# Subtracting the low half of the mixing stages' weights on VectorE alone

## The chip, the cores and the metric

The kernel runs on one core of one Trainium2 chip. The metric is the device time of one execution in microseconds (us). TensorE is called PE here, VectorE DVE, ScalarE ACT, GpSimd POOL, and SyncE, which issues most of the transfers, SP.

## The reference

A transformer-like backbone of two layers works on 128 context tokens and 512 latent tokens of width 1024. In each layer one large projection of the normalised input feeds four token mixers (a gated DeltaNet, differential attention, a gated linear recurrence, neighbourhood attention); their outputs are projected, gated, summed and projected again, and a SwiGLU block follows. Everything is float32:

```
h = _rmsnorm(x, lp['norm1_g']) * (1.0 + sc1) + sh1
mix, new_ctx = _token_mixers(h, lp, ctx)          # h @ w_in, four mixers, w_branch, gates, w_out
x = x + g1 * mix
h = _rmsnorm(x, lp['norm2_g']) * (1.0 + sc2) + sh2
x = x + g2 * _swiglu(h, lp['w_ffn_gate'], lp['w_ffn_up'], lp['w_ffn_down'])
```

## The kernel before

Activations lie with features on the 128 partitions and the 640 tokens along the free side, in halves of 320 (`HT`). The operands of the large products are split into a high part `hi` (cast to the type `F32R`) and a low part `lo = x - hi`, and each product is three matmuls: `hi*hi`, `hi*lo`, `lo*hi`.

For a weight this is done in `load_w`: SP issues the load of a tile of 128x1024 into `wraw` (2 buffers), ACT rounds it into `whi` (3 buffers), and the subtraction makes `wlo` (3 buffers). In the mixing stages (`self.weaving` is true) a full tile's subtraction is shared out: 608 columns on DVE, the last 416 (`PC`) on POOL. Everywhere else a full tile is done by DVE alone, but for the first three tiles of the program, which halve it (`pc=512`).

The mixing stage of each layer is woven. PE's instructions stand in an order that a planner writes out (`weave`): it has chains (`mix_a`, `prep_a`, `mix_c`, `mix_d`, `mix_b`, `prep_b`), each a generator that yields where PE has to wait for other engines, and a long list of projections (`fill`: `store_fm`, `store_tok`, `merge`, ...) with which it fills PE until the planner's clock says that a chain is ready. That clock (`now`, `charge`) counts the chains' work on each engine; the weights' subtraction is not counted in it. On DVE, ACT, POOL and SP the order within each engine is set by the framework's scheduler from priorities (`high_priority`; `load_w`'s split has `WPRI` 550000, a chain has 100000 times its rank counted from the back, up to 800000) and its own idea of durations. Each engine then runs its instructions strictly in that order.

Tile names that the text uses: `pu`, `ptk` are products of the projections; `cY`, `cZ`, `cQS`, `cRP`, `cAT`, `pca`, `pcb` belong to chain C (`c_head`); `cacc` is the short convolution of `prep_a`; `GX`, `GT`, `C`, `bm`, `bl`, `pkS`, `xp` belong to chain A; `rx`, `rr` to `prep_b`; `bpr`, `bcx`, `bqt`, `bKd` are loads of chain B that POOL issues; `lmn` is a single number of chain B; names that end in `rs_y` or `rs_t` are steps of a reciprocal root on a few columns. `prep_a`'s and `prep_b`'s transfers and chain B's go through memory, the latter two on POOL's queue.

Of the kernel before, what the change touches and what calls it, by code (L numbers as in the profile page):

```python
# [37 lines left out]
WPRI, WCUT = 550000, 1024  # L38
QB = 1
RE = 0  # L40
PC = 416
DPRI = 0
QM, QD = 1, 0
VC = 1
# [69 lines left out]
class Net:  # L114
# [163 lines left out]
    def load_w(self, src, n=1024, pc=0, raw=None):  # L278

        if raw is None:  # L280
            raw = self.wraw.tile([128, 1024], F32, tag="raw", name="wraw")
        with self.tc.high_priority(offset=DPRI):
            self.nc.sync.dma_start(raw[:, :n], src)
        hi = self.whl.tile([128, 1024], F32R, tag="hi", name="whi")
        lo = self.whl.tile([128, 1024], F32R, tag="lo", name="wlo", bufs=NLO)
        with self.tc.high_priority(offset=WPRI):
            m = n - (PC if self.weaving and n == 1024 else pc)
            self.a.copy(hi[:, :n], raw[:, :n])
            self.v.tensor_tensor(lo[:, :m], raw[:, :m], hi[:, :m].bitcast(F32), ALU.subtract)
            if m < n:  # L290
                self.g.tensor_tensor(lo[:, m:n], raw[:, m:n], hi[:, m:n].bitcast(F32), ALU.subtract)
        return hi, lo
# [1664 lines left out]
```

## Time and profile before

| | |
|---|---|
| median of 3 runs | 3494.56 us (3494.28 to 3498.4) |
| the profiled execution | 3495.59 us, of which 3493.6 us is the span from its first to its last instruction |
| PE busy | 3368.8 us (96%) |
| DVE busy | 2352.5 us (67%) |
| ACT busy | 1422.4 us (41%) |
| POOL busy | 544.5 us (16%) |
| mean granted clock of PE | 0.984 |

The mixing stage of the first layer lies from about 60 to 1240 us, that of the second from about 1780 to 3000 us; between and behind them stand the output projection and the SwiGLU blocks, in which POOL does nothing. PE is the engine to watch: its busy time is nearly the span, so a change shows where PE's idle time, or its time at the lower of its two clock levels (1.2 instead of 2.4 GHz, a granted clock of 0.5), grows or shrinks.

### The profile page before, as it was taken

The numbers are of one execution on the slowest core, as the hardware profiler recorded it, in microseconds if no ns is written. First come the engines' busy times: TensorE is split into PE (matmuls) and PEld (weight loads), VectorE is DVE, ScalarE is ACT, GpSimd is POOL, SyncE is SP. The second block draws the span as 40 slices with busy tenths as digits, with TensorE's granted clock in tenths as the row PEclk, the third lists the DMA queues.
The fourth block names the chain that finished last, engine by engine and source line by source line (L and its number), as shares of the span: only waits on it lengthen the run. The fifth ranks groups of instructions, "written<-read, shape, count | busy, mean of one in ns | idle before, by whom it ended". The sixth has DMA issues, their size and how long they took to land. (4 is left out here: it accounts for less than half of the span.)

```text
span 3493.6 us, 63588 instructions
## 1 busy us (share of the span) xinstructions
PE 3368.8 (96%) x23932; PEld 3298.6 (94%) x23932; DVE 2352.5 (67%) x5497; ACT 1422.4 (41%) x3170; POOL 544.5 (16%) x592
## 2 busy tenths in 40 slices
PE   8999999989999999999999999999999999999998
PEld 5989999988999999999999899999999999999998
DVE  7689888865676478887456797777555646633435
ACT  5344444544543353222253455445544433522222
POOL 2221112422122100000002212124122121000000
PEclk9999999999999999999999999999999999999999
DMA  6444333855454254444244333348453235322222
GB/s 218 151 145 139 115 110 124 242 178 159 131 154 126 95 177 147 151 153 131 76 131 148 130 115 112 103 127 244 141 150 120 87 100 161 106 67 79 74 84 67
DMA packets 297931, 460.16 MB, mean 132 GB/s; under 512 B 48148, under 2 KB 193172, under 8 KB 297624
## 3 DMA queue, kind: packets, MB, share of 16 engines
q1 hardware_dynamic: 286296, 423.58, 39.3%
q0 software_dynamic: 11328, 32.52, 3.1%
q8 instruction: 189, 3.10, 0.4%
q14 instruction: 118, 0.97, 0.1%
HBM read 368.42 MB, written 87.56 MB: 131 GB/s over the span
## 5 line engine op out<-in xcount | busy, mean ns | idle before, releaser
L152 PE MATMUL pu<-hh,whi 128*128 128x320 f32 (+1 forms) x3760 | 1094.7, 319 | 18.1 <-ACT stg L107 14.9
L152 PE MATMUL pu<-hl,whi 128*128 128x320 f32 (+1 forms) x3760 | 1064.8, 311 | 2.2 <-DVE hl L107 2.2
L152 PE MATMUL pu<-hh,wlo 128*128 128x320 f32 (+1 forms) x3760 | 1065.2, 311 | 0.0
L107 ACT CAST whi<-wraw 128x1024 fp32r<-128x1024 f32 (+2 forms) x410 | 391.1, 954 | 898.0 <-PE pu L152 492.6
L152 PEld LDWEIGHTS pu<-hh,whi 128*128 128x128 f32 (+1 forms) x3760 | 683.9, 189 | 23.3 <-ACT stg L107 15.7
L152 PEld LDWEIGHTS pu<-hl,whi 128*128 128x128 f32 (+1 forms) x3760 | 684.3, 189 | 4.5 <-DVE hl L107 2.5
L152 PEld LDWEIGHTS pu<-hh,wlo 128*128 128x128 f32 (+1 forms) x3760 | 682.5, 188 | 1.7
L107 DVE TENSOR_TENSOR wlo<-wraw,whi 128x608 fp32r<-128x608 f32 (+3 forms) x410 | 389.7, 951 | 314.2 <-ACT whi L107 309.4
L107 POOL TENSOR_TENSOR wlo<-wraw,whi 128x416 fp32r<-128x416 f32 (+1 forms) x209 | 325.5, 1558 | 1761.1 <-ACT whi L107 1539.8
L152 PE MATMUL pu<-mo,whi 128*128 128x320 f32 x1024 | 236.5, 318 | 5.4 <-DVE mo L107 3.4
L152 PE MATMUL pu<-fa,whi 128*128 128x320 f32 x1152 | 215.6, 309 | 0.0
L107 DVE SCALAR_TENSOR_TENSOR x<-pu,gn,x 128x128 f32<-128x128 f32 (+1 forms) x336 | 133.8, 435 | 93.3 <-PE pu L152 92.4
L152 PE MATMUL ptk<-whi,hh 128*128 128x256 f32 x640 | 193.9, 303 | 0.0
L512 DVE CUSTOM_DVE_ANT_0 junk<-wa,cs,mod 128x256 bf16<-128x256 f32 (+1 forms) x288 | 172.7, 600 | 25.6 <-DMA wa<-in_wada 20.7
L152 PE MATMUL ptk<-wlo,hh 128*128 128x256 f32 x640 | 183.5, 287 | 3.2 <-DVE wlo L107 3.2
L152 PE MATMUL ptk<-whi,hl 128*128 128x256 f32 x640 | 183.4, 287 | 0.0
L152 PEld LDWEIGHTS pu<-mo,whi 128*128 128x128 f32 x1024 | 174.5, 193 | 7.6 <-DVE mo L107 4.9
L152 PEld LDWEIGHTS pu<-fa,whi 128*128 128x128 f32 x1152 | 180.8, 188 | 0.0
L152 PE MATMUL pu<-mo,wlo 128*128 128x320 f32 x512 | 160.7, 314 | 0.0
L152 PE MATMUL pu<-fa,wlo 128*128 128x320 f32 x576 | 131.1, 309 | 0.0
L152 PEld LDWEIGHTS ptk<-wlo,hh 128*128 128x128 f32 x640 | 125.2, 196 | 3.4 <-DVE wlo L107 3.4
L152 PEld LDWEIGHTS ptk<-whi,hh 128*128 128x128 f32 x640 | 125.5, 196 | 0.0
(422 smaller groups left out, 6092.1 us busy)
## 6 DMA issues: line engine op xcount, KB each, us to landing
wraw<-in_win SPq DMA_DIRECT2D x151, 512.0 KB, 3.9
wa<-in_wada SPq DMA_DIRECT2D x116, 256.0 KB, 3.0
wraw<-in_wg SPq DMA_DIRECT2D x44, 512.0 KB, 3.5
wraw<-in_wu SPq DMA_DIRECT2D x44, 512.0 KB, 3.7
wraw<-in_wd SPq DMA_DIRECT2D x80, 256.0 KB, 2.6
p<-stg SPq DMA_DIRECT2D x112, 160.0 KB, 2.9
wa<-in_wada SPq DMA_DIRECT2D x128, 128.0 KB, 2.5
wraw<-in_wtok SPq DMA_DIRECT2D x32, 512.0 KB, 3.8
```

The source lines that it names most:

```text
L107: r = f(*args, **kw)
L152: r = self.nc.tensor.matmul(out, lhsT, rhs, start=start, stop=stop)
L512: self.nc.vector.tensor_tensor_reduce(junk, raw, cs[g], 0.5, o if k0 else self.bada[:, l, m:m + 1], ALU.mult, ALU.add, o)
```

## The change

The 416 columns go from POOL to DVE: in the mixing stages, DVE now subtracts all 1024 columns of a full tile in one instruction.

```
-PC = 416
...
-            m = n - (PC if self.weaving and n == 1024 else pc)
+            m = n - pc
             self.a.copy(hi[:, :n], raw[:, :n])
             self.v.tensor_tensor(lo[:, :m], raw[:, :m], hi[:, :m].bitcast(F32), ALU.subtract)
             if m < n:
                 self.g.tensor_tensor(lo[:, m:n], raw[:, m:n], hi[:, m:n].bitcast(F32), ALU.subtract)
```

207 instructions leave POOL, and 207 on DVE grow from 608 to 1024 columns. PE's order is the same, instruction for instruction. The scheduler, which counts a longer DVE instruction, orders the others anew: of 5499 instructions on DVE 1295 stand at another place (most by one to five places), of 2748 on ACT 300, of 1715 on SP 340.

POOL in the second layer, where it loads for the fourth head of chain B (`wlo` are the weights' low parts, the DMAs are issues of that head's loads). Before:

```order
313 L163 DMA bqt<-bqk_104 64x4x128 x2
314 L107 TENSOR_TENSOR wlo<-wraw,whi 128x416 x3
315 L163 DMA bqt<-bqk_104 64x4x128 x2
316 L107 TENSOR_TENSOR wlo<-wraw,whi 128x416 x5
317 L107 MEMSET bpr 128x256
318 L163 DMA bcx<-qk_97 128x128
319 L163 DMA bpr<-qk_97 64x128 x2
```

And now, at the same place:

```order
190 L162 DMA bqt<-bqk_104 64x4x128 x5
191 L106 MEMSET bpr 128x256
192 L162 DMA bcx<-qk_97 128x128
193 L162 DMA bpr<-qk_97 64x128 x2
194 L162 DMA bcx<-in_cvb 128x256
```

Nothing of the weights stands between the issues any more, here as everywhere in the mixing stages.

DVE in the second layer, at about 2035 us of the profiled execution, where chains A and C and the convolution are in flight together (the size of `cQS` and `cRP` tells chain C's level: 40x2x8 is one, 20x2x16 the next). Before:

```order
3287 L107 TENSOR_TENSOR C<-B,cst 128x512
3288 L107 TENSOR_TENSOR cZ<-cZ,cq 128x640
3289 L107 SCALAR_TENSOR_TENSOR cacc<-craw,cacc 128x642
3290 L107 TENSOR_TENSOR cQS<-cQS,cRP 128x40x2x8
3291 L107 TENSOR_TENSOR GT<-GT,pT 128x8x2x32
3292 L107 TENSOR_TENSOR GX<-GX,pX 128x8x2x32
3293 L107 TENSOR_TENSOR cRP<-cRP 128x40x2x8
3294 L107 TENSOR_TENSOR cY<-cY,cK 128x640
3295 L107 TENSOR_TENSOR cQS<-cQS,cRP 128x20x2x16
3296 L107 TENSOR_TENSOR cZ<-cZ,cq 128x640
3297 L107 TENSOR_SCALAR ams<-ass 128x5
```

And now:

```order
3289 L106 TENSOR_TENSOR C<-B,cst 128x512
3290 L106 TENSOR_TENSOR cY<-cY,cK 128x640
3291 L106 SCALAR_TENSOR_TENSOR cacc<-craw,cacc 128x642
3292 L106 TENSOR_TENSOR cZ<-cZ,cq 128x640
3293 L106 TENSOR_TENSOR GT<-GT,pT 128x8x2x32
3294 L106 TENSOR_TENSOR GX<-GX,pX 128x8x2x32
3295 L106 TENSOR_TENSOR cQS<-cQS,cRP 128x40x2x8
3296 L106 TENSOR_SCALAR cF<-cF,lbc,lb 128x640
3297 L106 TENSOR_TENSOR cRP<-cRP 128x40x2x8
3298 L106 TENSOR_SCALAR cF<-cF,lbc,lb 128x640
3299 L106 TENSOR_SCALAR ams<-ass 128x5
3300 L106 COPY_PREDICATED cAT<-cst,pca 128x512
```

Chain C has moved back by about a level: the `cY` and `cZ` that followed `cRP` 40x2x8 at once come some 15 places behind it now, while chain A's `GT` and `GX` stand where they stood.

## Rows read from the trace of the kernel before

**Rows 1.** Windows: stretch, length, then busy us (and instructions) of PE, PEld, DVE, ACT, POOL; granted clock; DMA

```profile
60.00:890.00 830.00, 777.70 (x5753) 758.93 (x5752) 648.17 (x1581) 389.70 (x908) 189.02 (x218) 0.97 0.50 152
890.00:1240.00 350.00, 347.22 (x2453) 343.37 (x2452) 228.65 (x638) 143.64 (x353) 73.91 (x69) 0.99 0.43 130
1780.00:2240.00 460.00, 443.68 (x3376) 432.79 (x3376) 337.76 (x672) 219.01 (x485) 90.63 (x101) 0.99 0.37 117
2240.00:3000.00 760.00, 733.06 (x5247) 722.96 (x5246) 471.59 (x1115) 344.75 (x832) 176.32 (x184) 0.98 0.47 140
2010.00:2090.00 80.00, 77.53 (x625) 76.26 (x623) 78.40 (x163) 45.11 (x102) 10.46 (x17) 1.00 0.36 116
```

**Rows 2.** Groups by form, DVE, whole span: xcount, busy us, mean ns, idle before

```profile
L107 DVE TENSOR_TENSOR wlo<-wraw,whi 128x608 fp32r<-128x608 f32 x207 | 189.9, 917 | 148.2 <-ACT whi L107 145.8 <-PE pdv L158 1.1 <-DMA wa<-in_wada 0.2
L107 DVE TENSOR_TENSOR wlo<-wraw,whi 128x1024 fp32r<-128x1024 f32 x119 | 145.6, 1223 | 125.0 <-ACT whi L107 123.0
L107 DVE SCALAR_TENSOR_TENSOR cacc<-craw,convw,cacc 128x642 f32<-128x642 f32 x96 | 95.3, 993 | 1.3
L107 DVE TENSOR_TENSOR b_s<-b_sp 128x1 f32<-128x1 f32 x64 | 18.6, 290 | 28.4 <-ACT be L107 28.2
```

**Rows 3.** Groups by form, DVE, from 1320 to 1780 us, where POOL is idle

```profile
L107 DVE TENSOR_TENSOR wlo<-wraw,whi 128x512 fp32r<-128x512 f32 x32 | 22.0, 686 | 7.3 <-ACT whi L107 7.1
```

**Rows 4.** Groups by form, POOL, whole span

```profile
L107 POOL TENSOR_TENSOR wlo<-wraw,whi 128x416 fp32r<-128x416 f32 x207 | 322.9, 1560 | 1759.7 <-ACT whi L107 1538.5 <-issue 33.0 <-DVE mrg L107 23.9
```

**Rows 5.** Timeline, DVE, 2030 to 2050 us: start us, duration us, instruction

```profile
2030.71 0.88 DVE L107 SCALAR_TENSOR_TENSOR cacc<-craw,convw,cacc 128x642 f32<-128x642 f32 x1
...
2038.31 0.82 DVE L107 TENSOR_TENSOR cRP<-cRP 128x640 f32<-128x640 f32 x1
...
2043.18 0.16 DVE L107 SCALAR_TENSOR_TENSOR ars_t<-ars_y 128x5 f32<-128x5 f32 x1
...
2044.93 0.82 DVE L107 TENSOR_TENSOR cY<-cY,cK 128x640 f32<-128x640 f32 x1
```

**Rows 6.** Timeline, first place: DVE, POOL and PE at 238 to 242 us

```profile
238.24 2.29 DVE L107 TENSOR_TENSOR cRP<-cRP 128x640 f32<-128x640 f32 x1
240.37 0.99 DVE L107 TENSOR_SCALAR grs_y<-grs_t 128x4 int32<-128x4 int32 x1
...
238.15 3.19 POOL L107 TENSOR_TENSOR wlo<-wraw,whi 128x416 fp32r<-128x416 f32 x2 [15.61 <-ACT whi L107]
...
242.09 0.39 PE L152 MATMUL ptk<-wlo,hh 128*128 128x256 f32 x1 [3.20 <-DVE wlo L107]
```

**Rows 7.** Timeline, second place: DVE, POOL and PE at 691 to 702 us

```profile
691.63 1.21 DVE L107 TENSOR_TENSOR rr<-rr,rot 128x1024 f32<-128x1024 f32 x1
...
696.61 2.08 DVE L107 TENSOR_TENSOR rx<-rx,rr 128x1024 f32<-128x1024 f32 x1
...
696.28 1.33 POOL L107 TENSOR_TENSOR wlo<-wraw,whi 128x416 fp32r<-128x416 f32 x1 [2.48 <-ACT whi L107]
...
701.48 0.63 PE L152 MATMUL pu<-hh,whi 128*128 128x320 f32 x1 [6.49 <-ACT stg L107]
```

**Rows 8.** Timeline, third place: POOL and PE at 2793 to 2801 us

```profile
2793.17 1.71 POOL L107 TENSOR_TENSOR wlo<-wraw,whi 128x416 fp32r<-128x416 f32 x1 [5.45 <-PE goT L158]
...
2800.09 1.13 PE L152 MATMUL pbs<-bpr,bcx 128*128 128x256 f32 x2 [2.60 <-DMA bpr<-qk]
```

**Rows 9.** Timeline, fourth place: DVE and PE at 2389 to 2399 us

```profile
2389.83 1.05 DVE L107 TENSOR_TENSOR lmn<-lmr 128x1 f32<-128x1 f32 x1
...
2398.43 0.64 PE L152 MATMUL pu<-hh,whi 128*128 128x320 f32 x1 [7.79 <-ACT stg L107]
```

**Rows 10.** Waits of PE: line, releaser, us in total, times, longest

```profile
PE pca L152 <- DVE ars_y L107: 2.6, 1, 2.6
PE pca L152 <- DVE cZ L107: 2.0, 1, 2.0
```

**Rows 11.** Timeline, PE at 2051 us

```profile
2051.62 1.05 PE L152 MATMUL pca<-cZ,cY 128*128 128x128 f32 x8
```

More of the change, by code (lines that the diff above doesn't have):

```diff
@@ L40 @@
 RE = 0
-PC = 416
 DPRI = 0
@@ L286, in load_w @@
         with self.tc.high_priority(offset=WPRI):
-            m = n - (PC if self.weaving and n == 1024 else pc)
+            m = n - pc
             self.a.copy(hi[:, :n], raw[:, :n])
```

## The prediction

> **What bounds the kernel now.** I read the windows of the mixing stages first, then the groups by form, the waits of PE and the timeline around PE's longest waits. The windows [rows 1] show PE at work nearly all the time: in the four stretches that make up the two mixing stages, 2400 us, it idles 52.3 + 2.8 + 16.3 + 26.9 = 98.3 us. Their granted clocks of 0.97, 0.99, 0.99 and 0.98 cost another 24.9 + 3.5 + 4.6 + 15.2 = 48.2 us of full speed. These 146 us are all that the change can give back, and what it can add to. The total of matmuls is untouched, and outside the mixing stages nothing changes. The same rows show who is close behind: DVE is busy 78% of the first stretch and 73% of the third, and 78.4 of 80 us from 2010 to 2090. POOL is busy a fifth to a quarter of the time. So the change takes work from an engine with room and gives it to the one that PE waits for; that is the case against it. The case for it is in how long the two engines' instructions take.
>
> **What DVE gains in work.** A full tile subtracted by DVE alone takes 1223 ns, one of 608 columns beside POOL's piece 917 [rows 2]: 306 ns more, 63.4 us for 207. But 917 isn't what 608 columns cost. Where POOL is idle, 512 columns take 686 ns [rows 3]; with 1024 at 1223 that is 1.05 ns a column, and 608 would take 787. So the gross addition is 436 ns x 207 = 90 us, of which 130 x 207 = 27 us is already spent, on waiting for POOL.
>
> **What DVE loses in waiting.** POOL's piece takes 1560 ns on average, 322.9 us in all [rows 4], and other DVE instructions beside it are stretched as well. A `cRP` step takes 0.82 us alone [rows 5] and 2.29 beside POOL's piece; a step on four or five columns takes 0.16 and 0.99 [rows 5, 6]; an addition of 1024 columns 2.08 us beside a POOL piece where its like takes 1.21 [rows 7]; one number 1.05 us [rows 9]. A hit costs 0.8 to 1.5 us. Over the span the group means show it: `cacc` 993 ns against 0.88 us alone, 96 x 0.11 = 10.5 us; `b_s`, one column, 290 against 0.16, 64 x 0.13 = 8.3 us [rows 2, 5]. Some of that is caused by POOL's other work, which stays. With the 27 us these two groups give 46 of the 90 back. The other 44 are made up if one POOL piece in four hits one more DVE instruction at 0.87 us. I can't add up all groups from rows, so DVE's net change lies between +44 us (nothing but these two groups) and well below zero. I take zero, since every place that I looked at closely has such a hit.
>
> The Trainium skill ("SBUF — State Buffer", section "Who interferes with whom") says that a DVE instruction with two SBUF inputs and a GpSimd instruction that reads SBUF exclude each other for their whole length, and that the order of issue decides which one waits. The stretched rows agree with that. By that rule a POOL piece holds DVE off even where no row here prices it; what this would give is the second rival.
>
> **What that does on the path.** DVE's sum matters less than where PE waits. I took four of PE's waits, of 3.20, 6.49, 2.60 and 7.79 us, 20.1 us together, and followed each back.
> First: PE needs a `wlo` that stands on DVE behind the stretched `cRP` and the stretched small step [rows 6]. Without POOL's piece these give back 1.47 + 0.83; the longer subtraction takes 0.44; 1.86 us less.
> Second: ACT's eviction stands behind a cast that waits for the stretched `rx` [rows 7]: 0.87 back, 0.44 more, 0.43 less.
> Third: PE waits for a load of `bpr`. POOL issues it, and its piece of 1.71 us stands directly ahead [rows 8]; in the new order nothing of the weights does. 1.71 us less; the bounds are 0 (if the buffer isn't free earlier) and the whole 2.60.
> Fourth: again an eviction on ACT, behind DVE's chain with the stretched `lmn` [rows 9]: 0.89 back, 0.44 more, 0.45 less.
> Together 4.45 of 20.1 us, 22%. I chose long waits, so this may flatter the change; short waits, on the other hand, often have one stretched instruction that is as long as they are.
> 22% of 98.3 us is 21.7 us. PE's order is fixed, and if PE gets to its next wait sooner, the chain it waits for isn't sooner ready unless its own path has become shorter. I give half of it back: 10.8 us stay. If waits shrink by 11%, I let the time at the lower clock, which sits behind the waits, shrink by as much: 5.3 us.
>
> **What moves.** PE's order is the same. DVE, ACT and SP have a new one. The weights' subtraction is not in the planner's clock, so the planner's places for PE don't follow. In the dense piece at 2035 us chain C's `cY` and `cZ` have slipped by some 15 places. Before, the last such `cY` ended at 2045.75 [rows 5] and the `pca` at 2051.62, which needs one of an earlier level, did not wait [rows 11]: several microseconds of room, so the slip alone need not reach PE. But `pca` has waited for DVE before, 2.6 and 2.0 us [rows 10], and I charge these a second time, 4.6 us. Bounds: 0, if the room suffices, and some 10, if it happens in both layers.
> `wraw` comes free when DVE is done, 436 ns later than DVE's part now, but a good 0.3 us sooner than POOL's 1560 ns; the load behind it on SP, and whatever stands behind that load, gains a little. I cost that at nothing: two buffers of `wraw` and three of `wlo` cover it, and without that cover it is again a gain. POOL's other work (`bm`, `GX`, the issues for chain B) no longer stands behind pieces that wait for ACT; costed at nothing but for the third place. ACT does the same casts.
>
> **The sum.** Against the profiled execution of 3495.6 us: -10.8 - 5.3 + 4.6 = -11.5. The median of the runs is 1.0 us lower than that execution, so from 3494.6 I come to **3483 us**, 0.33% less. What a measurement of this kernel can tell from no change is about 0.2%, 7 us.
>
> **Rivals.**
> *DVE becomes the bound (slower).* Only the two groups' stretch comes back, DVE has 44 us more to do, and in the stretches at 78% and 73%, which are 54% of the mixing time, half of that passes to PE, because PE's chains already wait for DVE there: 44 x 0.54 / 2 = 12, with the 4.6 of the order 17 us: 3511. For it: the 80 us with 1.6 us of free DVE time [rows 1], in which any longer instruction reaches the chains. It decides where DVE's free time in such a stretch is less than 0.44 us times its tiles. Against it: the stretched rows stand in just these chains.
> The Trainium skill ("Perfetto Trace Analysis", section "Optimizing Scalar/DVE Operations") allows moving work from a saturated DVE to GpSimd, and doubts in the same place that it helps between these two. Its first half is this rival; rows 6 to 9 speak for the second.
> *The exclusion is as strict as it can be (faster still).* If each POOL piece holds DVE for its own 1560 - 787 = 0.77 us, 159 us go for the 90 that come: DVE has 69 us less, and by the same two factors 19 us more reach PE: 3464. For it: hits of 0.8 to 1.5 us wherever I looked. Against it: the means of the groups, which give less.
> *The gain is handed on (no change).* The chains' waits shift to ACT, to transfers or to the next product of the same chain, and the fixed order of PE gives all of it back: within 7 us of 3494.6. For it: two of the four places end on ACT with only 0.4 us to win out of 6.5 and 7.8.
> That the change doesn't do what it says is excluded by the order: the 207 pieces are gone from POOL.
>
> **How the numbers follow.** The forecast (3474 to 3487.5) gets 0.35, the strict exclusion 0.12, no change 0.22, DVE as the bound 0.31. Faster by over 0.2% is then 0.47, within it 0.22, slower 0.31. The reshuffled order is what I can price least, so the slower case keeps much weight. The range goes from the strict exclusion's 3464 to just beyond the slower rival's time, 3512; the likeliest case alone would be 3474 to 3488.
>
> **What would show it.** Right: one group of `wlo` with 1024 columns, 326 of them at 1.22 us; `b_s` near 0.2 us and `cacc` near 0.9; DVE's busy time within some 20 us of 2352.5; POOL near 220 us; PE's waits at the four places shorter, the third most clearly. PE's idle time in the mixing stages below 90 us. Wrong: DVE busy 40 us more or beyond; PE's waits for `cZ`, `cY`, `GT` or `C` grown in the dense stretches; or a new long wait where the order was changed and no POOL piece had stood, which would mean that the shuffle and not the port decides the time.

## The result, and the profile after

The changed kernel takes **3445.18 us** (median of 5 runs, 3436.66 to 3447.1) where the one before takes 3497.53 (5 runs, 3494.28 to 3499.94): a ratio of 0.9848, 95% interval 0.9835 to 0.9861. That is 52 us less, where the prediction had 11 and its range ended at 3464. The direction was right, the size was out by a factor of four and a half.

The profiled execution took 3447.1 us. Its page begins (busy time, share of the span, instructions):

```profile
span 3445.3 us, 63065 instructions
PE 3350.5 (97%) x23932; PEld 3282.0 (95%) x23932; DVE 2340.3 (68%) x5497; ACT 1420.5 (41%) x3170; POOL 215.4 (6%) x385
```

The span is 48.3 us shorter than the 3493.6 of before. Of that, 18.3 us is PE's busy time (3368.8 before: the same matmuls, a little faster), and the other 30.0 is time in which PE stood still: 124.8 us before, 94.8 now. DVE's busy time fell by 12.2 us although it subtracts 207 x 416 columns more. POOL went from 544.5 to 215.4.

The windows that answer to [rows 1] (columns as there; the last one is shifted to the instructions of PE that stood at 2010 to 2090 us before, as PE is some 33 us ahead there):

```profile
60.00:890.00 830.00, 795.06 (x5965) 774.62 (x5964) 655.59 (x1642) 402.14 (x945) 81.58 (x151) 0.99 0.52 158
890.00:1240.00 350.00, 347.79 (x2463) 344.44 (x2462) 231.92 (x619) 142.95 (x336) 17.31 (x31) 1.00 0.43 131
1780.00:2240.00 460.00, 445.00 (x3423) 434.79 (x3422) 347.03 (x692) 220.03 (x482) 40.91 (x73) 0.99 0.38 121
2240.00:3000.00 760.00, 744.94 (x5318) 736.20 (x5317) 473.12 (x1117) 351.41 (x844) 60.98 (x109) 0.99 0.46 140
1977.00:2057.00 80.00, 74.45 (x591) 73.84 (x591) 77.19 (x161) 44.71 (x100) 5.87 (x12) 0.98 0.34 112
```

PE's idle time in the four stretches is 34.9 + 2.2 + 15.0 + 15.1 = 67.2 us, 31 less than before. One stretch got worse: in the last one PE now idles 5.6 us where it idled 2.5.

The groups of DVE that answer to [rows 2] (count, busy us, mean ns):

```profile
L106 DVE TENSOR_TENSOR wlo<-wraw,whi 128x1024 fp32r<-128x1024 f32 x326 | 401.3, 1231 | 269.2 <-ACT whi L106 262.6 <-DMA dqt<-dqk 3.3 <-DMA p<-stg 0.6
...
L106 DVE SCALAR_TENSOR_TENSOR cacc<-craw,convw,cacc 128x642 f32<-128x642 f32 x96 | 91.9, 957 | 1.4 <-DVE vn L106 0.2
...
L106 DVE TENSOR_TENSOR b_s<-b_sp 128x1 f32<-128x1 f32 x64 | 10.0, 156 | 27.4 <-ACT be L106 26.8
```

The full tile costs 1231 ns, as the 1223 of the prediction said, and `b_s` is back at its 0.16 us; `cacc` is at 0.96, since POOL's other work is still there (it is at 0.88 in the last run below, which takes that away).

### The profile page after: what moved, and what is told of

It reads as the page before. It is cut to its first block, busy times and chain, and to the rows that moved or that the text cites. A ratio compares the mean times of both kernels' runs of the same rounds, so it can differ in the third digit from the quotient of the medians.

```text
span 3445.3 us, 63065 instructions
## 1 busy us (share of the span) xinstructions
PE 3350.5 (97%) x23932; PEld 3282.0 (95%) x23932; DVE 2340.3 (68%) x5497; ACT 1420.5 (41%) x3170; POOL 215.4 (6%) x385
## 4 chain that ended last, share of the span: by engine, by line
PE 78%; DVE 9%; DMA 7%; issue 3%; ACT 2%; SPq 1%; POOL 0%; DVEq 0%; ACTq 0%; POOLq 0%
PE pu L151 58%; PE ptk L151 4%; DMA wa<-in_wada 2%; PE pdv L151 1%; PE pbo L151 1%; PE pbs L151 1%; PE pW L151 1%; DVE wlo L106 1%; PE pca L151 1%; PE pX L151 1%; PE pT L151 1%; DVE cacc L106 1%; PE pkS L151 1%; PE pao L151 1%; PE pdt L157 1%
## 5 line engine op out<-in xcount | busy, mean ns | idle before, releaser
L106 DVE TENSOR_TENSOR wlo<-wraw,whi 128x1024 fp32r<-128x1024 f32 (+2 forms) x410 | 455.6, 1111 | 308.8 <-ACT whi L106 302.0
L511 DVE CUSTOM_DVE_ANT_0 junk<-wa,cs,mod 128x256 bf16<-128x256 f32 (+1 forms) x288 | 165.2, 574 | 30.6 <-DMA wa<-in_wada 26.1
L106 DVE TENSOR_TENSOR fs<-fs,pu 128x320 f32<-128x320 f32 x88 | 39.6, 484 | 123.4 <-PE pu L151 123.3
```

The lines of the kernel that those rows point to most:

```text
L106: r = f(*args, **kw)
L511: self.nc.vector.tensor_tensor_reduce(junk, raw, cs[g], 0.5, o if k0 else self.bada[:, l, m:m + 1], ALU.mult, ALU.add, o)
```

## Experiments: what of POOL's piece costs the time

A piece did three things to others. It read two tiles beside DVE; it stood in POOL's queue ahead of other work of POOL, waiting there for ACT's cast; and it held `wraw` and `whi` until it was done. Three theories: the reading stretches DVE's instructions and that costs (1); the order that the scheduler made for the change is simply better (2); POOL's queue or the held tiles cost (3). The expectations use these numbers. In every experiment PE's order is the same as before, but for the two that move POOL's remaining reads.

**POOL reads again, for nobody.** On top of the changed kernel:

```
+ for i in (0, 208):
+     h = hi[:, i:i + 208].bitcast(F32)
+     self.g.tensor_tensor(self.scr, raw[:, i:i + 208], h, ALU.subtract)
```

> The changed kernel, with GpSimd given back its reading: per weight tile of the mixing stages two subtractions of 208 columns read raw and hi and write a scratch tile that nobody reads, while VectorE still subtracts all 1024 columns. The order of the instructions on VectorE differs in 172 of 5499 from the changed kernel's, TensorE's in none. Theory 1 (VectorE's instructions are stretched when GpSimd reads beside them, and that was what filled the idle time of before): the stretch of before comes back on top of VectorE's longer share, one group of the low parts at 1.3 us or more instead of 1.231, the other VectorE operations again about 70 us longer in all, VectorE busy near 2430 us, and the time at 3490 to 3530 us, at or above the kernel before. Theory 2 (the new order of the instructions made the gain): 3440 to 3455 us. Theory 3 (GpSimd's queue, in which the pieces stood ahead of DMA issues and masks, made the gain): 3480 to 3500 us, with VectorE's durations unchanged.

3525.84 us against 3498.7 (ratio 1.0088, 1.0065 to 1.011). The whole gain is gone and 27 us more. The order (2) is not what gained: it was kept almost entirely.

**POOL only writes.**

```
+ for _ in range(6):
+     self.g.memset(self.scr, 0.0)
```

> The changed kernel, with GpSimd's queue filled again but without reads: per weight tile of the mixing stages six memsets of 208 columns of a scratch tile that nobody reads, some 1.6 us together. The order of the instructions on VectorE, ScalarE, SyncE and TensorE is the changed kernel's to the last one. Theory 1 (reads of GpSimd stretch VectorE): 3440 to 3455 us, VectorE busy near 2340 us. Theory 3 (the queue of GpSimd): 3475 to 3500 us. If the memsets stretch VectorE too, VectorE's busy time says so by 50 us or more. Theory 2 (the order) expects 3440 to 3455 us as theory 1 does.

3513.71 us against 3498.7 (1.0041, 1.0026 to 1.0057), and that with VectorE's busy time at 2339.1, as in the changed kernel. This looks like theory 3, but the profile says that the run tested something else. POOL's line of the page (busy tenths in 40 slices of the span), and the windows of this run and of the changed kernel:

```profile
POOL 8888810120010000000000001002010100000000
30.00:480.00 450.00, 380.68 (x2688) 359.10 (x2686) 312.52 (x746) 178.96 (x408) 357.53 (x1226) 0.93 0.39 124
480.00:890.00 410.00, 392.61 (x2937) 385.19 (x2936) 326.90 (x821) 208.50 (x488) 50.25 (x85) 0.99 0.56 168
```

```profile
30.00:480.00 450.00, 427.12 (x3181) 408.23 (x3181) 376.38 (x885) 213.45 (x475) 38.66 (x73) 0.99 0.45 142
480.00:890.00 410.00, 392.12 (x2904) 383.74 (x2903) 305.97 (x818) 207.20 (x515) 52.24 (x88) 0.99 0.59 175
```

The memsets wait for nothing, so the scheduler set them far ahead of their tiles, and they fill POOL's queue up to 480 us: PE stands still 46 us longer there, at a clock of 0.93 instead of 0.99, and no longer after that. It shows that a full queue of POOL costs PE dearly, but a piece of the kernel before never stood like that.

**Before, without the reading.** First with one memset in the place of the subtraction, then with POOL's queue and occupancy kept nearly as they were:

```
- self.g.tensor_tensor(lo[:, m:n], raw[:, m:n], hi[:, m:n].bitcast(F32), ALU.subtract)
+ self.g.memset(lo[:, m:n].bitcast(F32), 0.0)
```

> The kernel before, with VectorE's 608 columns and its order (11 of 5499 instructions on VectorE stand elsewhere), but GpSimd writes zeros into the other 416 columns of the low part instead of subtracting: the low part of those columns is left out. Theory 1: without the reads VectorE's other operations lose their 72 us of stretch and the low parts 27 us, VectorE busy near 2260 us, and the time at 3425 to 3445 us, below the changed kernel, since the 90 us of subtraction that this saves lie in idle time only in part. Theory 2 (the order is what gained): 3480 to 3500 us, since this is the order of before. Theory 3 (the queue): between, as the pieces are 0.5 us instead of 1.56.

3447.81 us against 3498.7 (0.9854, 0.9835 to 0.9873), just above what theory 1 had here.

```
+ k = m + 8
+ self.g.tensor_tensor(lo[:, m:k], raw[:, m:k], hi[:, m:k].bitcast(F32), ALU.subtract)
+ for _ in range(3):
+     self.g.memset(lo[:, k:n].bitcast(F32), 0.0)
```

> The kernel before with GpSimd's queue, waits and occupancy kept but its reading taken away: of the 416 columns of a tile GpSimd subtracts 8 (so that the piece still waits for hi and raw), then writes zeros into the other 408 three times, some 1.4 us a tile against 1.56; the low part of those 408 columns is left out. VectorE's order is before's except for 82 of 5499 instructions. Theory 1 (GpSimd's reads stretch VectorE): 3440 to 3460 us, as in the run with one memset a tile (3447.8), and VectorE's other operations without the 72 us of stretch. Theory 3 (the pieces stand in GpSimd's queue ahead of DMA issues, masks and copies, and wait there for ScalarE): 3480 to 3500 us, as this queue is before's. Theory 2 (the order) is down already by the run with one memset a tile.

3446.9 us against 3499.33 (0.9845, 0.9829 to 0.986). Page line and POOL's two groups of the second run:

```profile
PE 3353.5 (97%) x23932; PEld 3285.4 (95%) x23932; DVE 2267.4 (66%) x5497; ACT 1419.9 (41%) x3170; POOL 592.9 (17%) x1213
L107 POOL MEMSET wlo<- 128x408 f32 x621 | 276.1, 445 | 1634.7 <-PE pu L152 1324.6 <-PE ptk L152 273.8 <-DMA craw<-p 15.7
L107 POOL TENSOR_TENSOR wlo<-wraw,whi 128x8 fp32r<-128x8 f32 x207 | 108.8, 526 | 41.1 <-ACT whi L107 39.0 <-DVE a_g L107 1.3
```

POOL is busy 592.9 us, more than before, and the order of nearly all instructions of the other engines is before's; still 52 us are gone. The queue is nearly before's: the memsets don't need `whi`, so they wait for PE to be done with the old `wlo` (1324.6 + 273.8 of 1634.7 us of idle time) where the piece had waited for ACT's cast, and the 8 columns follow. What stands behind them still waits (this run's rows are among those on `dPl` below). So without the reading, and with `wraw` free earlier, 52 us go although the queue stays, and the new order isn't needed for it. What an empty queue would give beside 608 columns on DVE, no run shows.

**The reading or the held tiles.** Without the reading, `wraw` also came free earlier. Two runs take these apart; both start from the kernel before. The first subtracts 8 columns, writes 400 twice, and subtracts the last 8 (held longer, hardly read); the second subtracts 8 and then reads constants (read as much, not held):

```
+ u = bc1(self.Ui[:, :102], 4)
+ self.g.tensor_tensor(lo[:, k:n].rearrange("p (t c) -> p t c", t=4), u, u, ALU.subtract)
```

> The kernel before, with GpSimd holding raw and hi as long as before but hardly reading: of its 416 columns it subtracts the first 8, writes zeros into 400 twice, then subtracts the last 8; the low part of the 400 is left out. VectorE's order is before's except for 40 of 5499 instructions. If the late release of raw (and so the next load) is what costs: 3480 to 3500 us. If the reading beside VectorE is: 3445 to 3460 us (two short subtractions a tile, each able to hold an instruction of VectorE up once, may add some us to the 3446.9 of the run without the hold).

> The kernel before, with GpSimd reading as much as before but nothing that anybody waits for: of its 416 columns it subtracts 8, and fills the other 408 with the difference of a constant and itself, two inputs and as many columns as before; raw and hi come free after the 8. The low part of the 408 is left out. VectorE's order is before's except for 11 of 5499 instructions. If the reading beside VectorE is what costs: 3490 to 3510 us, with VectorE's other operations stretched by some 70 us again. If the late release of raw is: 3447 to 3460 us, and VectorE's stretch, which comes back all the same, lies where it has time.

Held: 3452.33 us against 3497.33 (0.9868, 0.9842 to 0.9893). Read: 3480.76 (0.9955, 0.9939 to 0.9971), between the two cases that I had written. Holding the tiles costs some 7 us, which the intervals don't tell from nothing. It is not the whole hold, either: in this run too the memsets go ahead of the subtractions, and SP's queue waits 42.5 us for POOL's pieces, where it waited 95.3 before and 15.4 in the run without the hold. Reading constants brings back 36 us, with 54 us of stretch instead of the 72 expected; the constant pieces are shorter too, 0.87 us where nothing of DVE lies beside them against 1.08.

**The dose.** Half the columns on POOL (`PC = 208`), and one input instead of two (`tensor_scalar(lo, raw, 0.0, None, mult)` on 408 columns beside 8 that are subtracted):

> The kernel before with 208 columns on GpSimd instead of 416: VectorE takes 816. Half the reading, so theory 1 expects about half of the way: 3462 to 3480 us, with the low part's group near 1.05 to 1.1 us. Theory 2 has no figure to offer, since 1002 of 5499 VectorE instructions stand elsewhere than before; 3445 us or 3495 us would speak for it. Theory 3 expects about two thirds of the gain, as a piece of 208 columns is over half as long as one of 416: 3460 to 3470 us.

> The kernel before, with GpSimd reading one tile instead of two: of the 416 columns of a tile it subtracts 8, so that the piece still waits for hi and raw, and sets the other 408 to raw times zero in one operation; their low part is left out. VectorE's order is before's except for 11 of 5499 instructions. Theory 1 says that reads of GpSimd stretch VectorE and leaves open how many at a time it takes. If one read does as two: 3485 to 3500 us, with some 70 us of stretch on VectorE's other operations. If only an operation with two inputs does it: 3440 to 3455 us, as the run with writes alone (3446.9). If half: 3465 to 3480 us.

3463.01 us for half the columns (0.9901, 0.9882 to 0.9919), 3468.47 for one input (0.9913, 0.9894 to 0.9932). The first lies in the ranges of theories 1 and 3 alike and doesn't tell them apart. From each trace I added up by how much DVE's other instructions exceed the median of their own form with nothing of POOL beside, where a piece lies beside them:

```
kernel                       stretch us   time against before, us
before                          72.0          0
reads constants                 54.1        -16.6
208 columns                     29.2        -35.7
one input                       22.2        -29.7
8 columns and memsets           11.6        -52.4
the same, held                   9.3        -45.0
one memset                       3.8        -50.9
the changed kernel               1.1        -52.4
```

The time follows the stretch at about 0.7 us for each, within some 9 us. The low parts' own stretch is not counted in it (22 us before; with it the change would have 52 us of time for 94 of stretch, 0.55 each). Why the changed kernel stands on the same line, with some 75 us more of DVE's time than the three kernels above it, is the next question.

## Experiments: what the added work and POOL's queue are worth

On top of the changed kernel I gave POOL back its queue alone, and then its reading alone. A first attempt read constants that waited for nothing:

> The changed kernel with GpSimd reading beside VectorE again, but constants: per weight tile of the mixing stages 8 columns of raw and hi are subtracted into a scratch tile (so that it begins when hi is there), then two operations of 200 columns with two constant inputs write the scratch tile; nobody reads it. VectorE's order is the changed kernel's except for 13 of 5499 instructions. If the reading costs by the stretch of VectorE's other operations alone: some 40 to 55 us of stretch, and 0.7 of it in time, 3470 to 3490 us. If the reading costs more once VectorE has all 1024 columns: 3510 to 3530 us, as with raw and hi held. If the late release of raw and hi made the whole loss there: 3445 to 3455 us.

3623.01 us (1.0361, 1.0338 to 1.0384), and it says nothing on the question: the constant operations bunched in the first 360 us as the memsets had (PE's instructions are 164 us late by 425 us, and 13 us more at the end). Tied to the 8 columns ahead of them, they stand where the pieces stood:

```
+ self.g.tensor_tensor(self.scr[:, :8], raw[:, :8], hi[:, :8].bitcast(F32), ALU.subtract)
+ for _ in range(6):
+     self.g.memset(self.scr[:, :200], 0.0)
```

and, for the reading, in the place of the memsets

```
+ u = bc1(self.Ui[:, :100], 2)
+ for _ in range(2):
+     self.g.tensor_tensor(self.scr[:, :200].rearrange("p (t c) -> p t c", t=2), u, u, ALU.subtract)
```

> The changed kernel with GpSimd's queue filled as long but without reading: the same 8 columns, then six memsets of 200 columns of the scratch tile, tied to the 8 ahead of them, some 1.6 us a tile. VectorE's order is the changed kernel's except for 97 of 5499 instructions. If reading is what costs: 3445 to 3460 us. If the queue is: 3475 us or more.

> The changed kernel with GpSimd reading constants beside VectorE: per weight tile of the mixing stages 8 columns of raw and hi are subtracted into a scratch tile, then two operations of 200 columns with two constant inputs write the same columns again, so that they can't run ahead of the 8; nobody reads the tile. VectorE's order is the changed kernel's except for 73 of 5499 instructions. If the reading costs by the stretch of VectorE's other operations alone (0.7 us of time for each us): 3465 to 3490 us. If it costs more once VectorE has all 1024 columns: 3510 to 3530 us. If the late release of raw and hi made the loss of the earlier run: 3445 to 3455 us.

Writing: 3468.14 us against 3501.57 (0.9914, 0.9892 to 0.9936). Reading: 3493.32 (0.9981, 0.997 to 0.9993). The first lies between the two cases that I had written: with DVE's other stretch as in the changed kernel (23.7 us by all of POOL's work, 25.4 there), the queue costs 19 us. Some of that can be `wraw`, for whose release by the 8 columns SP's queue waits 64.6 us in that run. The reading on top costs 25 more, at 40 us of stretch. The very first run, 3525.8, costs 35 more than the one with constants. DVE is busy 21 us longer there (2409.3 against 2388.2), which at 0.7 each is 15 of the 35. The tiles are held behind DVE's longer subtraction, too: SP's queue waited 151 us for those pieces there, 30.5 in the run with constants. That is the likeliest ground for the rest; no run shows it apart.

So the change has **three terms**, each run taken against the kernel before of its own chip: reading gone, and `wraw` free earlier with it, -52 (8 columns and memsets); 416 more columns on DVE in the order that the scheduler made for them, with the queue still full, +19 (the run with writing stands at -33.4); queue empty, -19 (the changed kernel at -52.4). The intervals of these runs are some 5 to 8 us wide to each side, so each 19 may be out by some 9. The two later terms are nearer to upper bounds, as a piece of the run with writing takes POOL 2.5 us and one of before 1.6.

What the queue does can be seen at one wait of PE, for `dPl` of chain D. POOL and PE before, then in the changed kernel, then in the run with writing, and PE in the run of before with 8 columns and memsets (start, duration, instruction, idle time before it and what ended it; below, the loads of `dbias`, issue to landing):

```profile
854.26 1.69 POOL L107 TENSOR_TENSOR wlo<-wraw,whi 128x416 fp32r<-128x416 f32 x1 [7.07 <-ACT whi L107]
855.90 0.57 POOL L163 DMA_DIRECT2D bcx<-in_cvb  x1
856.46 1.25 POOL L163 DMA_DIRECT2D bqt<-bqk  x2
857.70 1.11 POOL L163 DMA_DIRECT2D bKd<-bqk  x2
858.80 1.26 POOL L163 DMA_DIRECT2D bqt<-bqk  x2
867.89 1.11 PE L158 MATMUL pdt<-cst,dPl 128*128 128x128 f32 x4 [6.53 <-ACT dPl L107]
DMA to landing us min/median/max: 4.6/8.5/8.8
```

```profile
803.74 1.24 POOL L162 DMA_DIRECT2D bqt<-bqk  x2
808.90 0.56 POOL L162 DMA_DIRECT2D bKd<-bqk  x1 [3.92 <-PE pdv L151]
809.79 0.55 POOL L162 DMA_DIRECT2D bKd<-bqk  x1 [0.34 <-PE pdv L151]
827.42 1.25 POOL L162 DMA_DIRECT2D bqt<-bqk  x2 [17.07 <-ACT oTq L106]
838.78 0.65 PE L157 MATMUL pdt<-cst,dPl 128*128 128x128 f32 x4 [0.83 <-ACT dPl L106]
DMA to landing us min/median/max: 4.0/4.2/4.5
```

```profile
832.73 1.23 POOL L106 TENSOR_TENSOR scr<-wraw,whi 128x8 f32<-128x8 f32 x1 [5.89 <-ACT whi L106]
833.91 0.57 POOL L162 DMA_DIRECT2D bcx<-in_cvb  x1
844.99 1.12 PE L157 MATMUL pdt<-cst,dPl 128*128 128x128 f32 x4 [4.96 <-ACT dPl L106]
DMA to landing us min/median/max: 4.7/7.1/9.4
```

```profile
843.28 1.12 PE L158 MATMUL pdt<-cst,dPl 128*128 128x128 f32 x4 [5.48 <-ACT dPl L107]
DMA to landing us min/median/max: 8.9/9.0/9.0
```

Before, a piece waits 7.07 us for ACT's cast, and seven issues of chain B stand behind it. They go out in one burst from 855.9 us, just as SP issues `dbias` (857.4 and 859.3): it lands after more than 8 us, chain D waits, and PE with it, 6.53 us. In the changed kernel most of these issues are out by 810.3 us, 22 us ahead of the `dbias` of 832.4; it lands in 4.2 us, and PE waits 0.83. With the queue filled again, both come back, and in the last run, which has lost POOL's reading and nearly kept its queue, both had stayed. PE's waits for `dPl` at `pdt` sum to 15.3 us before, 3.6 after, 13.8 with the queue filled, and 9.8 in the last run.

## Experiments: is a gain handed back, and can the order be mended

The prediction gave half of every gain back. So the change was made in part of the tiles:

```
- m = n - (PC if self.weaving and n == 1024 else pc)
+ m = n - pc
+ if self.weaving and n == 1024:
+     self.nt = getattr(self, "nt", 0) + 1
+     if self.nt > 52:
+         m = n - PC
```

with `PC = 416` put back, and `> 52` for the change in the first 52 tiles, `> 105` for layer 0 alone and `<= 105` for layer 1 alone.

> The kernel before, with the change in the first 52 weight tiles of the mixing stages alone (they end near 660 us); after them GpSimd takes its 416 columns again. By then the changed kernel is some 20 us ahead of the one before in TensorE's instructions. If what one place gives is kept (the waits behind it are as long as they were): about 20 us less, 3475 to 3482 us, and the lead stands through the rest of the trace. If half is handed back, as the prediction had it, because TensorE reaches the next wait sooner: 10 us less, 3486 to 3491 us, the lead shrinking behind 660 us. If all: 3495 to 3500 us.

> The kernel before, with the change in layer 0 alone (105 of 207 weight tiles). The changed kernel was 32.7 us ahead at the end of layer 0's mixing stage. If that is kept: 3463 to 3470 us, and the lead stands through layer 1. If half is handed back in layer 1: 3480 us or more.

> The kernel before, with the change in layer 1 alone (102 of 207 weight tiles). If the layers add: 48 less the 32.7 us of layer 0, so about 16 us less than before, 3478 to 3486 us, and TensorE's instructions level with before's up to 1780 us. If layer 1 gained in the changed kernel only because layer 0 had arrived in another state: 3490 us or more.

First 52 tiles: 3478.96 us against 3498.17 (0.9934, 0.991 to 0.9958). Layer 0: 3469.33 (0.9911, 0.989 to 0.9932). Layer 1: 3475.53 (0.9928, 0.991 to 0.9946). The layers' gains, 28.8 and 22.6, add up to 51.4. How far the same instruction of PE is ahead of before, in us, from the traces:

```
before at        598     955    1302    1834    2493    3022 us
changed        -19.1   -29.4   -32.7   -30.7   -35.8   -48.6
first 52       -22.3   -20.5   -20.6   -21.3   -17.3   -15.3
layer 0        -20.8   -30.7   -32.9   -33.2   -28.6   -28.9
layer 1          0.7     4.3     4.5     2.6    -2.8   -19.7
```

What the first 52 tiles gain stands through the rest of layer 0, in which the old pieces are back. In layer 1 both runs that enter it early lose some of their lead, 4 us of 33 and 6 of 21; but the run that leaves layer 0 as before strays by 4.5 us in layer 0, so that much may be chance. By the times nothing is handed back (51.4 against the 52.4 of the whole change).

**The order.** Two waits of PE for `cZ` looked like the price of the new order. Three rows for the first, before, in the run with one memset and in the changed kernel, and one for the second, in the changed kernel:

```profile
670.21 2.08 PE L152 MATMUL pca<-cZ,cY 128*128 128x128 f32 x8 [1.96 <-DVE cZ L107]
657.56 1.65 PE L152 MATMUL pca<-cZ,cY 128*128 128x128 f32 x6 [6.08 <-DVE cZ L107]
655.68 2.08 PE L151 MATMUL pca<-cZ,cY 128*128 128x128 f32 x8 [5.19 <-DVE cZ L106]
2028.11 1.97 PE L151 MATMUL pca<-cZ,cY 128*128 128x128 f32 x8 [4.42 <-DVE cZ L106]
```

The first isn't new. It stands before too, 1.96 us, and is longer still in the run with one memset, which has before's order but for 11 instructions: PE comes to it some 17 us sooner there, chain C only 13. Here a gain is handed on, as the prediction thought. The second is new: none of the runs with before's order of DVE in layer 1 has it, and all those with the changed kernel's do, at 3.6 to 4.4 us.

I let the splits rank behind chain C (`WPRI` 450000), and moved POOL's remaining reads away (the copies into `GX` and `GT` to ACT; with them `bm` and `bl` to DVE):

> The changed kernel with one priority moved: the splits of the weights rank behind chain C instead of ahead of it (WPRI 450000 instead of 550000), which puts 705 of 5499 VectorE instructions elsewhere, the cY and cZ of chain C ahead of splits among them. If the two new waits of TensorE for cZ (5.2 and 4.4 us) are the price of the new order, they go, and nothing takes their place: 3430 to 3438 us. If the split that now stands behind is waited for instead, or another chain: 3440 to 3455 us.

> The changed kernel with the 40 copies into GX and GT on ScalarE instead of GpSimd (24 us of GpSimd's work that reads beside VectorE). If what is left of the stretch of VectorE (about 28 us by all of GpSimd's other work) still holds TensorE up at the rate of the change (48 us less span for about 95 us less stretch), taking some 12 us of it away gives 3436 to 3442 us. If it lies where VectorE has time, 3443 to 3450 us; if ScalarE's copies come late behind its own work, more.

> The changed kernel with the copies into GX and GT on ScalarE and the three mask operations (bm, bl) on VectorE, so that GpSimd keeps DMA issues and memsets. At the rate of the change, about 25 us less stretch against some 20 us more work of VectorE's own: 3430 to 3442 us. If the stretch that is left lies where VectorE has time, or if the order that moves with it (TensorE's too) costs as much: 3443 to 3460 us.

3451.7 us (0.9861, 0.9845 to 0.9877), 3445.4 (0.9844, 0.9828 to 0.9861), 3450.81 (0.9857, 0.9842 to 0.9872): none is better than the change. With the splits behind, the wait at 2028 is gone, the one at 655 is still 4.87 us, and a product now waits for its low part instead:

```profile
2019.19 0.64 PE L151 MATMUL pu<-hh,wlo 128*128 128x320 f32 x1 [3.60 <-DVE wlo L106]
```

With all of POOL's reads gone, 2.9 us of DVE's stretch are left of 25, and nothing is won. What POOL still does beside DVE may lie where DVE has time, but the runs don't show it: PE's order moves in both that take POOL's reads away, and in the last it makes waits of 7.95, 9.22 and 10.59 us of its own.

## Why the prediction was right and where it was wrong

*What bounds the kernel* held: everything was won in the mixing stages [rows 1], and the lead doesn't change outside them.

*DVE's work and stretch cancel* held as a sum: DVE is busy 12 us less, where I took zero, and the stretch that was to make up for 90 us of added work was there (72 on other instructions, 22 on the low parts). What I missed is that the two are not worth the same. A microsecond of stretch costs 0.7 us of time by the table above; the added columns cost 19 for 90, 0.2 each, the new order included, presumably since they lie on tiles that are prepared ahead. Netting the two on DVE hid the difference.

*The four places* gave 11.4 of 20.1 us instead of 4.45. The rows that answer to [rows 6, 7, 9]:

```profile
233.81 1.40 DVE L106 TENSOR_TENSOR cRP<-cRP 128x640 f32<-128x640 f32 x1
235.06 0.16 DVE L106 TENSOR_SCALAR grs_y<-grs_t 128x4 int32<-128x4 int32 x1
236.38 0.38 PE L151 MATMUL ptk<-wlo,hh 128*128 128x256 f32 x1 [1.91 <-DVE wlo L106]
```

```profile
680.61 1.21 DVE L106 TENSOR_TENSOR rx<-rx,rr 128x1024 f32<-128x1024 f32 x1
681.19 0.42 PE L151 MATMUL pu<-hh,whi 128*128 128x320 f32 x1 [0.58 <-ACT stg L106]
```

```profile
2355.44 0.14 DVE L106 TENSOR_TENSOR lmn<-lmr 128x1 f32<-128x1 f32 x1
2360.17 0.64 PE L151 MATMUL pu<-hh,whi 128*128 128x320 f32 x1 [6.20 <-ACT stg L106]
```

First: 1.29 instead of 1.86; `grs_y` is at 0.16 as said, but this `cRP` takes 1.40 with no instruction of POOL beside it (its columns lie otherwise than in [rows 5]), so I took 0.58 us of stretch too much. Second: 5.91 instead of 0.43 (a wait of 1.69 returns at the next such product, at 705.6); `rx` is at 1.21 as said, but the chain came earlier by more than this one step, which was all that I had counted; which steps those are, I didn't follow. Third [rows 8]: 2.60, no wait is left; I had taken 1.71. Fourth: 1.59 instead of 0.45, with `lmn` at 0.14. The 0.44 us charged for the longer subtraction came true at the first place, where PE waits for that very low part (0.89 + 0.83 - 0.44 = 1.28); over all 207 tiles the added columns cost 19 us, 0.09 each. **Counting one or two stretched steps of a chain, and charging the added work at every place**, is the first step that failed: idle time in the mixing stages fell by 31 us (32%), with the longer waits for `cZ` already in it, not by 21.7.

*Half is handed back* is the second: by the three runs on parts of the tiles it is nothing by their times, and 4 us of 33 and 6 of 21 by their traces. It happens at single places, as at the wait for `cZ` at 655 us.

*The clock shrinks by 11%* is the third: 5.3 us were forecast and PE's busy time fell by 18.3. The time at the lower clock doesn't follow the sum of the waits but the long ones. Windows of before and after around the wait for `dPl` (stretch, length, busy us of PE, PEld, DVE, ACT, POOL, then the granted clock):

```profile
861.00:867.80 6.80, 0.35 (x3) 0.09 (x1) 1.64 (x9) 1.02 (x5) 0.00 (x0) 0.78 0.91 229
867.90:871.30 3.40, 3.40 (x14) 3.40 (x15) 1.33 (x4) 2.60 (x6) 0.56 (x1) 0.50 0.36 99
```

```profile
833.00:838.70 5.70, 3.52 (x22) 3.21 (x22) 3.71 (x16) 3.06 (x11) 0.00 (x0) 1.00 0.66 214
838.80:842.20 3.40, 3.40 (x24) 3.40 (x25) 1.94 (x4) 2.40 (x6) 0.00 (x0) 1.00 0.36 102
```

Behind the wait of 6.53 us PE works 3.4 us at 0.50, which is the level of 1.2 GHz. In the changed kernel, where PE pauses 1.52 and 0.83 us there, the clock is 1.00 throughout. Waits over 2 us fell from 20 to 13 and from 70.4 to 43.3 us in sum; that is 27 of the 30 us of idle time, and it took low stretches away whole: the clock records of the traces have 21 of them before, 115 us together, and 13 after, 67 us.

*What moves*: 4.6 us for the order were charged, with some 10 as the bound. PE's waits of `pca` for `cZ` and `ars_y` went from 4.6 [rows 10] to 11.7 us, 7.1 more, between the two. The new wait of 4.4 us is the part that the order made, so the charge was about right, and the rest is handed on. The prediction had such a new wait as a sign that the shuffle decides the time; it came, and the time fell all the same. No run got rid of these waits without another in their place. *POOL's other work costed at nothing but for the third place* is the fourth step that failed: it is worth up to some 19 us, give or take 9. `wraw`'s release at nothing was about right as far as the runs show it (some 7 for part of the hold, not told from nothing).

*The rivals.* DVE as the bound had its price about right, 12 us for 44 of added work where 19 for 90 were measured, but set it against a gain that was far too small. The strict exclusion came nearest with 3464, but not by its own mechanism: DVE's busy time fell by 12 us and not by 69. The 1560 ns that it took for POOL's own piece hold POOL's waiting for DVE as well (1082 with nothing of DVE beside). The gain handed on is refuted as a whole.

## What to carry to other kernels

Work that is moved off GpSimd is not to be netted against the engine that takes it: here the stretch of VectorE's instructions, on the chains that TensorE waits for, was worth 0.7 of its length, and the bulk work added to tiles that are prepared ahead 0.2. Look at what stands behind a waiting piece in GpSimd's queue, transfers above all: they come late and all at once. What fills an engine's queue in an experiment must wait for what the original waited for, or the scheduler bunches it at the start.

## What the runs showed of the hardware

**Two inputs exclude, one seldom holds anything up.** One addition of DVE (`mrg`, 0.49 us alone) beside POOL's piece with two inputs before, beside one with two constant inputs, and beside one with a single input:

```profile
1211.79 1.35 DVE L107 TENSOR_TENSOR mrg<-mrg,mth 128x320 f32<-128x320 f32 x1
1211.13 1.67 POOL L107 TENSOR_TENSOR wlo<-wraw,whi 128x416 fp32r<-128x416 f32 x1 [5.99 <-ACT whi L107]
```

```profile
1179.11 0.72 DVE L107 TENSOR_TENSOR mrg<-mrg,mth 128x320 f32<-128x320 f32 x1
1178.62 0.87 POOL L107 TENSOR_TENSOR wlo<-cst 128x408 fp32r<-128x408 f32 x1 [5.84 <-issue]
```

```profile
1121.71 0.49 DVE L107 TENSOR_TENSOR mrg<-mrg,mth 128x320 f32<-128x320 f32 x1
1121.30 1.23 POOL L107 TENSOR_SCALAR wlo<-wraw 128x408 fp32r<-128x408 f32 x1 [8.03 <-issue]
```

Beside two inputs it ends 0.34 us after the piece, both times; beside one input both run at their own speed, in all 13 such pairs of that trace (POOL's piece began first in 12). It isn't free in all. Of 54 two-input instructions of DVE of 0.35 us or more that began behind a piece with one input, 8 took over 0.1 us longer than alone, by 0.3 in the mean; before, beside two inputs, it was 43 of 72, by 0.6. Short instructions of DVE that are held up there lose 0.2 to 0.4 us, against 0.3 to 0.9 beside two inputs. The two runs with memsets have DVE's low parts at 799 and 812 ns, 12 and 25 above what 608 columns take alone. It goes the other way too: with 208 columns on POOL a piece takes 631 ns where nothing of DVE lies beside it (three pieces) and 1447 in the median, 816 more, of the 1.00 us that 816 columns take on DVE (worked out from [rows 2, 3]).

The Trainium skill ("SBUF — State Buffer", section "Who interferes with whom") has a VectorE instruction with two SBUF inputs contend with a GpSimd instruction that reads SBUF, under an exclusive lock, and not with one that only writes. For two inputs (the pairs at 1.35 and 0.72) and for writes (DVE's busy time is 2339.1 us with 1242 memsets and 2340.3 without) these runs agree; for a single input (the 13 pairs at 0.49) they don't. One of the stretched rows that the prediction had agree with it isn't a case of it: `grs_y` [rows 6] reads one tile and took 0.99 us all the same, where it takes 0.16 now.

**Fewer inputs are not faster.** POOL's operation with one input takes 1235 ns for 408 columns where nothing of DVE lies beside it (eight pieces), the one with two 1082 for 416 (three). The run with one input stands 23 us behind the one with memsets although its stretch is only 11 us more. By 0.7 us for each that is 7 to 8, holding `wraw` longer may be another 7, and the rest stays open.
